# Attention with the probabilities scaled by 1/sum ahead of their transposes, in a two-layer hybrid transformer kernel

## The chip, the cores and the metric

One Trainium2 chip, one core of it. The metric is device time in microseconds (us) of one execution; of several runs the median is given. The engines are named as in the profile: PE (TensorE, with its weight loads as PEld), DVE (VectorE), ACT (ScalarE), POOL (GpSimd), and SP (SyncE, which issues the DMAs).

## The reference

Two layers over 1024 latent tokens (a 16 x 64 grid) and 256 context tokens of 1024 features, all in float32. The first layer mixes with neighbourhood attention (8 heads of 64) and a gated linear recurrence, the second with gated linear attention and grouped-query attention (8 query heads of 64 on 2 key heads). What the change touches are the two softmax attentions:

```python
# neighbourhood attention: 8 rows of keys around the query's row, 16 columns, and all of the context
p = softmax(concat([s_loc, s_ctx]))         # s_loc has the relative bias, -inf outside the window
o = einsum(p_loc, v_rows) + einsum(p[n_loc:], v_c)
# context queries of the first layer: the context alone
pc = softmax(q_c @ k_c.T * scale);  o_c = pc @ v_c
# grouped-query attention: context and all latents
p = softmax(q @ k.T * scale);  o = p @ v
```

## The kernel before

Products of float32 operands are made from two halves: each operand is a sum hi + lo in a short form, and a product is three matmuls (`mm3`, lines 128 to 133) or, in attention, two. The projections, with 512 columns per matmul, are most of the time.

Attention works in units of one head and 128 queries (`AttnUnit`). Neighbourhood attention has 80 of them: per head two of context queries, with 256 keys, and eight of latent queries, with 768 or 896 keys (four each). Grouped-query attention has 64, each with 1024 latent and 256 context keys. A unit goes through these methods:

- `scores` (L714): six or fewer matmuls into PSUM; VectorE copies the scores to SBUF (tiles `sc`) with the running maximum (L850 to L871, or L1519 and L1521).
- `exp` (L723): ScalarE takes the exponential in place and adds up the row sums into the small tile `st`.
- `norm` (L728, L729): VectorE adds the two sums where there are two tiles, and takes the reciprocal into `st[:, 7:8]`.
- `turn` (L738): TensorE transposes the probabilities, 128 keys each, into PSUM, up to four to a bank. With the last bank it also transposes the reciprocal, spread over 128 columns (L740), so that 1/sum lies along the columns; ScalarE copies that to SBUF (L741) into one of four buffers `rb` of the pool `recip`. ScalarE and VectorE then write the transposed probabilities as hi + lo into `pt` (L751, L752). For the third bank of every second unit of grouped-query attention the lo half is made by GpSimd (L747 to L749).
- `values` (L758): TensorE multiplies `pt` with the values, hi and lo of both, into one PSUM bank for two query tiles (`Pair`).

`run_attention` is a software pipeline over the units. In one step it issues the scores of unit n, `norm` of unit n-1, whatever closes an earlier pair, `turn` of unit n-3, `exp` of unit n, `values` of unit n-4, and then one step of the background generators and of a filler. The filler in both stages is the early half of the output projection: its weights are split on ScalarE and GpSimd (L90, L92), its matmuls run on TensorE (L131 to L133), and GpSimd adds its results to the residual (L1143), which goes back to DRAM. In neighbourhood attention GpSimd also adds masks to each next head's bias tables (L681, L684) ahead of the norm of the step in which they are issued; the tables come by DMA (L652).

`attn_out` closes a pair: ScalarE copies and VectorE adds the halves of the four partial products (L800, L801), GpSimd adds the two of each tile (L803, 64x256) and multiplies each tile by its 1/sum (L809, two of 64x128). In neighbourhood attention latent queries lie in reversed column order (`flip`), and the product writes them back in order.

Every engine works through its own instructions in the order in which the program issues them.

Of the kernel before, what the change touches and what calls it, by code (L numbers as in the profile page):

```python
# [10 lines left out]
F32 = mybir.dt.float32  # L11
# [20 lines left out]
class Emit:  # L32
    def __init__(self, ctx, tc, A, out, dbg):
# [7 lines left out]
        self.rp = e(tc.tile_pool(name="recip", bufs=4))  # L41
# [53 lines left out]
    def w_ahead(self, n_split, n_dma):  # L95
        """Keep n_split units split, and n_dma more loaded, beyond the units taken."""
        end = len(self.wplan)
        while self.wsp < min(end, self.wpos + n_split):
            self.w_load(self.wsp + 1)
            self.w_split(self.wsp)  # L100
            self.wsp += 1
        upto = min(self.wsp + n_dma, self.wpos + n_split + n_dma)

        def later():
            for _ in range(self.w_lag):
                yield
            self.w_load(upto)

        if self.w_lag:
            self.bg.append(later())  # L110
        else:
            self.w_load(upto)
# [15 lines left out]
    def mm3(self, ps, w, u, start, stop):  # L128
        """ps += w.T @ u with both operands given as (hi, lo)."""
# [5 lines left out]
    def split(self, hi, lo, src, scale=None, pool=False):  # L135
        """hi + lo = src (times a power of two): hi by ScalarE, lo by VectorE or GpSimd."""
# [9 lines left out]
class Act:  # L146
    """Feature-major activations in (hi, lo): per 128 features, tokens 1024 + 256."""
# [20 lines left out]
class Res:  # L168
    """Feature-major float32: per 128 features a [128, 1024] tile, and 256 more."""
# [40 lines left out]
def params(E):  # L210
    """Vectors over features: loaded as rows, turned into columns of one tile."""
# [35 lines left out]
class Mods:  # L247
    """mod[l][:, j] = (silu(c), silu(c_ctx)) @ w_mod[l][:, 1024 j:] + b_mod, features on partitions.

    A pass covers 1024 columns: ("b", l, j) a block, or ("h", l, hf) half hf of blocks 0 and 1."""  # L250
# [86 lines left out]
def make_gain(E, l, which, a, b):  # L337
    """gain = norm_w * (1 + scale)"""
# [9 lines left out]
def mod_part(E, src, r, u, k, c, gain, shift, pool=False):  # L348
    """u(hi, lo) = src * r * gain + shift, as a generator."""
# [17 lines left out]
def start(E):  # L367
    """x, ctx: row sums of squares, transposes, modulation and the norm of layer 0; x.T goes to DRAM."""
# [61 lines left out]
def proj_fm(E, w, u, cs, done):  # L430
    """Feature-major product of one 128-column unit w (hi, lo: [128, 8, 128]) for chunks cs.

    A generator of four steps per chunk; done(c, n, ps) may return a generator, run in the background."""
# [13 lines left out]
def col_units(key, ap, c0, n):  # L447
    """n units of 128 columns of a [1024, *] weight."""
# [12 lines left out]
def tick(E):  # L461
    """One step of every background generator."""
# [5 lines left out]
def store(E, dst, src, lag=4):  # L468
    """A store that is issued some background steps later, when its data is there."""
# [12 lines left out]
def pipe(gens, gap):  # L482
    """Software pipeline: a generator starts every gap steps, all started ones advance by one per step."""
# [54 lines left out]
def lru_tile(E, j, xl, gl, ct, o_d):  # L538
    """Conv, gates, both recurrences and the output gate of channels 128 j .. 128 j + 127."""
# [87 lines left out]
def na_bias_setup(E):  # L627
    """rpb rows padded to 127 columns in DRAM, so that a [64, 64] Toeplitz block is one strided read."""
# [14 lines left out]
def na_head_load(E, h, qk_d, v_d):  # L643
    """Bias tables and operands of head h."""
# [31 lines left out]
def na_head_mask(E, hd, i):  # L676
    """Quarter i of the masks of a head's bias tables."""
# [14 lines left out]
class AttnUnit:  # L692
    """One 128-query tile of one head.

    qs: (hi, lo) stationary operands [128, 128]; pieces: PSUM tiles of scores, each a list of moving APs;
    soft(pss, ss, st) writes the scores and returns a function that gives -max; groups: columns of each score tile;
    vtiles: stationary [128 keys, vh | vl] per key tile; o_ps() gives the PSUM columns of the output."""
# [27 lines left out]
    def norm(self):  # L725
# [3 lines left out]
        nc.vector.reciprocal(st[:, 7:8], st[:, 5:6])  # L729
        self.cols = [s[:, o:o + 128] for s, n in zip(self.ss, self.groups) for o in range(0, n, 128)]  # L730
        self.pts = []

    def turn(self, b):
# [5 lines left out]
        if b == self.nb - 1:  # L739
            nc.tensor.transpose(ps[:, m * 128:m * 128 + 128], self.st[:, 7:8].to_broadcast([128, 128]), E.ident)  # L740
            nc.scalar.copy(self.o_ps.recip(), ps[:, m * 128:m * 128 + 128])  # L741
# [20 lines left out]
def run_attention(E, units, fill=None, lag=3):  # L762
    """Software pipeline over the units of an iterator: norm 1, turn lag, values lag + 1 steps after the scores."""
# [30 lines left out]
def attn_out(E, pair, parity, dst, flip=False):  # L794
    """dst[64 rows at 64 * parity, two query tiles] = the four partial products of pair.ps [128, 2, 2, 128], times pair.r."""
# [7 lines left out]
    nc.gpsimd.tensor_tensor(v[:, :, 0], v[:, :, 0], v[:, :, 1], op=OP.add)  # L803
    for i in range(2):
        w, r, d = v[:, i, 0], pair.r[i][a], dst[:, i * 128:i * 128 + 128]
        if flip:
            w, r, d = (x.rearrange("p (r q) -> p r q", q=64) for x in (w, r, d))
            d = d[:, :, ::-1]
        nc.gpsimd.tensor_tensor(d, w, r, op=OP.mult)  # L809


class Pair:
    """The outputs of two query tiles in PSUM, and 1 / sums along their columns; taken at the first use."""

    def __init__(self, E):
        self.E, self.ps, self.r = E, None, {}
# [5 lines left out]
class Part:  # L822
# [8 lines left out]

    def recip(self):
        p = self.pair
        p.r[self.i] = p.E.rp.tile([128, 128], F32, name=p.E.nm("rb"), tag="rb")
        return p.r[self.i]
# [130 lines left out]
def mixer0(E, u, st, tail):  # L966
    """st: what is left of the norm that writes u; tail(O, h): what follows chunk 2."""
# [124 lines left out]
class Back:  # L1092
    """The residual read back from DRAM: ctx() its chunk 2, lat() chunks 0 and 1 of 128 features more."""
# [16 lines left out]
def faster(g, n):  # L1110
    """n steps of g as one."""
# [11 lines left out]
def out_plan(E, l, w, early, late, cs):  # L1123
    """Weights of an out projection, 256 columns at a time: rows from 128 * early once per chunk, then the others."""
# [6 lines left out]
def out_early(E, l, cs, load, back):  # L1131
    """h += gate * (O @ w_out) in DRAM, for the four feature tiles of O that load(c) brings; a generator.

    The sums are read back (back) once they are all there."""
# [55 lines left out]
def out_proj(E, l, O, h, c, W, fill, norm, ahead=0):  # L1190
    """h += gate * (O @ w_out) for chunk c and the four feature tiles of O; steps of fill run in between; a generator.

    norm, the norm of the result, takes a step after every tile of 128 features. ahead, for the last chunk: how many
    of the weights that follow are split meanwhile."""
# [26 lines left out]
def norm_mod(E, h, u, c, gain, shift, pool=False, lag=2, which=0):  # L1221
    """u = norm(h) * gain + shift for chunk c, as a generator; the first eight steps take h.part(0..7)."""
# [30 lines left out]
def ff_ops(cs, G=2):  # L1253
    """Order of the products of the hidden groups g: (1 or 2, group, chunk).

    Two chunks: two groups of the first one come first. Three chunks: the second one starts early. The last
    two groups end chunk 0 early."""
# [46 lines left out]
def ff(E, l, u, h, ops, G=2, fill=None, after=None, woven=False, slow=None, split=False):  # L1304
    """h += gate * (relu(u @ w1)^2 @ w2), as the given ops; fill, slow: run in between.
# [881 lines left out]
```

## Time and profile before

| | |
|---|---|
| median of 3 runs | 2994.69 us (2993.69 to 2995.0) |
| span of the profiled execution | 2993.8 us |
| TensorE busy | 2898.8 us (97%) |
| VectorE busy | 1605.6 us (54%) |
| ScalarE busy | 1195.7 us (40%) |
| GpSimd busy | 1076.7 us (36%) |
| neighbourhood attention | about 403 to 655 us of the span |
| grouped-query attention | about 1920 to 2242 us |

The profile is taken on one execution; its span runs from the first to the last instruction. Busy shares are means over stages with different limits, so the views by stretch say more than the page's totals. Durations of TensorE's instructions overlap; what an instruction takes of TensorE's time is read from one start to the next. In rows of groups, "x" is the count; behind the bar come the busy time in us and the mean in ns of one, and then the idle time before them with what ended it.

### The profile page before, as it was taken

To read this page: it belongs to the slowest core of one execution; us is meant where nothing else is said; L and a number is where in the kernel's file an instruction comes from. 1 tells how busy PE (TensorE), PEld (TensorE's weight loads), DVE (VectorE), ACT (ScalarE), POOL (GpSimd) and SP (SyncE) were. 2 spreads that over 40 slices of the span, in tenths; PEclk is the share of its full clock that TensorE was granted. 3 is DMA by queue.
4 is the path that set the end of the run, shared out by engine and by line. 5 is a ranking of instruction groups with operands and counts; after the bars stand their busy time and mean duration, and the time that the engine had idled before them with its cause. 6 is when DMAs were issued, how large, how long until landed. Compare 5 with 4: busy or idle time off the path is not lost. (4 is left out here: it accounts for less than half of the span.)

```text
span 2993.8 us, 43072 instructions
## 1 busy us (share of the span) xinstructions
PE 2898.8 (97%) x16517; PEld 2500.8 (84%) x16517; DVE 1605.6 (54%) x3309; ACT 1195.7 (40%) x2301; POOL 1076.7 (36%) x866
## 2 busy tenths in 40 slices
PE   7999999989999999999999998899999999999998
PEld 5797789978888888888888797789988888888887
DVE  5454458877434534534437566888886332323334
ACT  5654458864211112112125343578884112112122
POOL 1443347643332222223234334325545233323230
PEclk9999999999999999999999999999999999999999
DMA  7235698831221221321213221334411111111111
GB/s 253 86 113 193 222 246 230 232 97 43 71 64 50 71 78 51 105 71 57 84 43 125 86 78 39 103 106 139 142 45 58 43 57 43 57 43 50 49 57 57
DMA packets 235173, 286.98 MB, mean 96 GB/s; under 512 B 32656, under 2 KB 172760, under 8 KB 234968
## 3 DMA queue, kind: packets, MB, share of 16 engines
q1 hardware_dynamic: 234968, 284.24, 30.9%
q8 instruction: 130, 2.13, 0.3%
q14 instruction: 75, 0.61, 0.1%
HBM read 226.97 MB, written 57.23 MB: 95 GB/s over the span
## 5 line engine op out<-in xcount | busy, mean ns | idle before, releaser
L131 PE MATMUL ps<-act,whi 128*128 128x512 f32 (+1 forms) x2176 | 805.1, 370 | 6.5 <-ACT act L355 5.4
L132 PE MATMUL ps<-act,whi 128*128 128x512 f32 (+1 forms) x2176 | 800.5, 368 | 0.8 <-POOL act L361 0.7
L133 PE MATMUL ps<-act,wlo 128*128 128x512 f32 (+1 forms) x2176 | 798.6, 367 | 2.1 <-POOL wlo L92 1.2
L92 POOL TENSOR_TENSOR wlo<-wst,whi 128x1024 fp32r<-128x1024 f32 x190 | 465.7, 2464 | 408.6 <-ACT whi L90 282.6
L139 DVE TENSOR_TENSOR hid<-t,hid 128x512 fp32r<-128x512 f32 (+1 forms) x160 | 102.3, 639 | 793.1 <-ACT hid L138 793.1
L131 PEld LDWEIGHTS ps<-act,whi 128*128 128x128 f32 x2176 | 412.9, 190 | 78.3 <-issue 7.4
L131 PE MATMUL ps<-hid,whi 128*128 128x512 f32 (+1 forms) x1296 | 476.2, 367 | 0.0
L132 PE MATMUL ps<-hid,whi 128*128 128x512 f32 (+1 forms) x1296 | 474.4, 366 | 0.0
L133 PE MATMUL ps<-hid,wlo 128*128 128x512 f32 (+1 forms) x1296 | 474.2, 366 | 0.0
L133 PEld LDWEIGHTS ps<-act,wlo 128*128 128x128 f32 x2176 | 412.0, 189 | 70.5 <-POOL wlo L92 1.6
L132 PEld LDWEIGHTS ps<-act,whi 128*128 128x128 f32 x2176 | 412.9, 190 | 65.5 <-POOL act L361 1.3
L1345 POOL TENSOR_TENSOR t<-t 128x512 f32<-128x512 f32 (+1 forms) x160 | 153.7, 960 | 865.6 <-ACT t L1344 857.5
L1344 ACT ACTIVATE t<-ps 128x512 f32<-128x512 f32 (+1 forms) x160 | 88.7, 555 | 922.2 <-PE ps L133 922.1
L1363 DVE SCALAR_TENSOR_TENSOR hl<-ps,mod,hl 128x512 f32<-128x512 f32 (+1 forms) x520 | 371.0, 738 | 134.3 <-PE ps L133 131.2
L131 PEld LDWEIGHTS ps<-hid,whi 128*128 128x128 f32 x1296 | 245.1, 189 | 41.6 <-issue 1.6
L133 PEld LDWEIGHTS ps<-hid,wlo 128*128 128x128 f32 x1296 | 245.0, 189 | 39.6
L132 PEld LDWEIGHTS ps<-hid,whi 128*128 128x128 f32 x1296 | 245.2, 189 | 38.9
L90 ACT CAST whi<-wst 128x1024 fp32r<-128x1024 f32 x194 | 197.9, 1048 | 82.9 <-PE ps L132 37.6
L723 ACT ACTIVATE sc<-sc,st 128x1024 f32<-128x1024 f32 (+3 forms) x208 | 178.1, 859 | 32.2 <-DVE st L1524 23.8
L752 DVE TENSOR_TENSOR pt<-ps,pt 128x512 fp32r<-128x512 f32 (+2 forms) x304 | 169.1, 598 | 18.9 <-ACT pt L751 16.4
L751 ACT CAST pt<-ps 128x512 fp32r<-128x512 f32 (+2 forms) x304 | 153.4, 526 | 37.2 <-PE ps L738 29.8
L138 ACT CAST hid<-t 128x512 fp32r<-128x512 f32 (+1 forms) x160 | 92.5, 578 | 184.3 <-POOL t L1345 184.3
(326 smaller groups left out, 4187.9 us busy)
## 6 DMA issues: line engine op xcount, KB each, us to landing
wst<-in_w_ff SPq DMA_DIRECT2D x128, 512.0 KB
wm<-in_w_mod SPq DMA_DIRECT2D x96, 512.0 KB
wst<-in_w_in_even SPq DMA_DIRECT2D x20, 512.0 KB
wst<-in_w_in_odd SPq DMA_DIRECT2D x18, 512.0 KB
qk_d<-qks SPq DMA_DIRECT2D x16, 512.0 KB
wst<-in_w_out_even SPq DMA_DIRECT2D x16, 512.0 KB
qst<-qk_d SPq DMA_DIRECT2D x32, 256.0 KB
he<-h_d SPq DMA_DIRECT2D x32, 256.0 KB
```

The costliest lines, as they stand in the source:

```text
L90: self.nc.scalar.copy(hi, st)
L92: engine.tensor_tensor(lo, st, hi.bitcast(F32), op=OP.subtract)
L131: t.matmul(ps, w[0], u[0], start=start, stop=False)
L132: t.matmul(ps, w[0], u[1], start=False, stop=False)
L133: t.matmul(ps, w[1], u[0], start=False, stop=stop)
L138: self.nc.scalar.copy(hi, src)
L139: (self.nc.gpsimd if pool else self.nc.vector).tensor_tensor(lo, src, hi.bitcast(F32), op=OP.subtract)
L723: self.E.nc.scalar.activation(s, s, AF.Exp, bias=self.nm, accum_out=self.st[:, 5 + i:6 + i])
L751: nc.scalar.copy(pt[:, :, 0], src)
L752: nc.vector.tensor_tensor(pt[:, :, 1], src, pt.bitcast(F32)[:, :, 0], op=OP.subtract)
L1345: nc.gpsimd.tensor_tensor(r, r, r, op=OP.mult)
L1363: nc.vector.scalar_tensor_tensor(dst, ps[:, :n], gate[:, o, v:v + 1], dst, op0=OP.mult, op1=OP.add)
```

## The change

`norm` gets one GpSimd instruction per score tile, which multiplies the exponentials in place by the unit's 1/sum, one value per partition. The transposes then work on scaled probabilities. The broadcast transpose of the reciprocal (L740), its copy (L741), the buffers for it and `Part.recip` go. `attn_out` no longer multiplies: where the columns are in order, GpSimd's add of the two partial products of both tiles writes the output; where they are reversed, two adds, one for each tile, write it in order. The rest of the diff removes comments.

```diff
-        self.rp = e(tc.tile_pool(name="recip", bufs=4))
...
         nc.vector.reciprocal(st[:, 7:8], st[:, 5:6])
+        for s in self.ss:
+            nc.gpsimd.tensor_scalar(s, s, st[:, 7:8], None, op0=OP.mult)
         self.cols = [s[:, o:o + 128] for s, n in zip(self.ss, self.groups) for o in range(0, n, 128)]
...
-        if b == self.nb - 1:
-            nc.tensor.transpose(ps[:, m * 128:m * 128 + 128], self.st[:, 7:8].to_broadcast([128, 128]), E.ident)
-            nc.scalar.copy(self.o_ps.recip(), ps[:, m * 128:m * 128 + 128])
         pt = E.S([128, m, 2, 128], F32R, name="pt")
...
     v = t[a].rearrange("p (u s q) -> p u s q", u=2, s=2)
-    nc.gpsimd.tensor_tensor(v[:, :, 0], v[:, :, 0], v[:, :, 1], op=OP.add)
+    if not flip:
+        nc.gpsimd.tensor_tensor(dst.rearrange("p (u q) -> p u q", u=2), v[:, :, 0], v[:, :, 1], op=OP.add)
+        return
     for i in range(2):
-        w, r, d = v[:, i, 0], pair.r[i][a], dst[:, i * 128:i * 128 + 128]
-        if flip:
-            w, r, d = (x.rearrange("p (r q) -> p r q", q=64) for x in (w, r, d))
-            d = d[:, :, ::-1]
-        nc.gpsimd.tensor_tensor(d, w, r, op=OP.mult)
+        x, y, d = (z.rearrange("p (r q) -> p r q", q=64) for z in (v[:, i, 0], v[:, i, 1], dst[:, i * 128:i * 128 + 128]))
+        nc.gpsimd.tensor_tensor(d[:, :, ::-1], x, y, op=OP.add)
...
-    def recip(self):
-        p = self.pair
-        p.r[self.i] = p.E.rp.tile([128, 128], F32, name=p.E.nm("rb"), tag="rb")
-        return p.r[self.i]
```

## Rows read from the trace of the kernel before

**Rows 1.** The page: busy time of TensorE, and the chain that ended last by line.

```profile
PE 2898.8 (97%) x16517; PEld 2500.8 (84%) x16517; DVE 1605.6 (54%) x3309; ACT 1195.7 (40%) x2301; POOL 1076.7 (36%) x866
PE 32%; DVE 3%; issue 0%; ACT 0%; POOL 0%; DMA 0%; SPq 0%; DVEq 0%; POOLq 0%; ACTq 0%
```

**Rows 2.** Busy us (x instructions) of each engine by stretch, with granted clock and DMA.

```profile
core 0: us, PE busy (x) PEld busy (x) DVE busy (x) ACT busy (x) POOL busy (x), PEclk, DMA share, GB/s
425.00:590.00 165.00, 163.04 (x1206) 154.28 (x1205) 137.99 (x519) 141.77 (x334) 121.00 (x143) 1.00 0.90 233
...
2003.00:2166.00 163.00, 162.93 (x1093) 148.81 (x1094) 141.65 (x432) 140.78 (x329) 82.45 (x95) 1.00 0.43 133
2166.00:2210.00 44.00, 42.98 (x311) 38.89 (x309) 43.43 (x151) 42.65 (x106) 16.48 (x26) 1.00 0.23 67
```

**Rows 3.** The same view of the broadcast transposes (L740) alone: PE, PEld, clock, DMA.

```profile
425.00:590.00 165.00, 14.99 (x55) 7.53 (x55) 1.00 0.90 233
...
2003.00:2166.00 163.00, 9.00 (x33) 4.57 (x34) 1.00 0.43 133
2166.00:2210.00 44.00, 3.27 (x12) 1.60 (x12) 1.00 0.23 67
```

**Rows 4.** Timeline of the weight loads in grouped-query attention: start, us, instruction.

```profile
2101.80 0.14 PEld L740 LDWEIGHTS ps<-ident,st 128*128 128x128 f32 x1
2101.91 0.42 PEld L758 LDWEIGHTS ps<-pt,vl 128*128 128x128 f32 x3
```

**Rows 5.** Groups by line over the whole span: removed product and removed copy.

```profile
L809 POOL TENSOR_TENSOR ol<-t,rb 64x128 f32<-64x128 f32 x128 | 57.0, 464 | 5.0
...
L741 ACT COPY rb<-ps 128x128 f32<-128x128 f32 x144 | 39.8, 276 | 16.2 <-POOL oc L809 6.2 <-PE ps L740 5.2 <-POOL ol L809 4.1
```

**Rows 6.** Groups by line of GpSimd from 425 to 590 us.

```profile
L92 POOL TENSOR_TENSOR wlo<-wst,whi 128x1024 fp32r<-128x1024 f32 x10 | 24.0, 2396 | 6.4 <-ACT whi L90 6.3
...
L803 POOL TENSOR_TENSOR t<-t 64x256 f32<-64x256 f32 x27 | 19.8, 734 | 31.3 <-DVE t L801 26.0 <-ACT rb L741 4.4 <-POOL b L681 0.4
...
L684 POOL TENSOR_TENSOR braw<-braw,m 128x512 f32<-128x512 f32 x11 | 14.3, 1304 | 0.1
```

**Rows 7.** Groups by line of GpSimd over the span, three of 128x1024.

```profile
L92 POOL TENSOR_TENSOR wlo<-wst,whi 128x1024 fp32r<-128x1024 f32 x190 | 465.7, 2464 | 408.6 <-ACT whi L90 282.6 <-issue 46.1 <-DVE acc L285 32.4
...
L1697 POOL TENSOR_TENSOR ss<-ss,dec 128x1024 f32<-128x1024 f32 x4 | 7.6, 1896 | 22.8 <-DVE ss L1691 19.2 <-PE ps L133 3.5
...
L1966 POOL MEMSET att<- 128x1024 f32 x1 | 1.0, 957 | 0.0
```

**Rows 8.** Timelines: a unit's reciprocal and its transposes, in each attention.

```profile
500.84 0.16 DVE L729 RECIPROCAL st<-st 128x1 f32<-128x1 f32 x1
...
506.10 0.92 PE L738 MATMUL ps<-ident,sc 128*128 128x128 f32 x7
...
2107.08 0.16 DVE L729 RECIPROCAL st<-st 128x1 f32<-128x1 f32 x1
...
2115.59 1.26 PE L738 MATMUL ps<-ident,sc 128*128 128x128 f32 x10
```

**Rows 9.** Waits of ScalarE from 403 to 650 us: total, times, longest.

```profile
ACT rb L741 <- POOL oc L809: 6.2, 4, 2.4
...
ACT rb L741 <- POOL ol L809: 4.1, 6, 1.1
```

**Rows 10.** Timelines: a mask that waited for its table, and transposes after it.

```profile
418.78 0.88 POOL L681 TENSOR_TENSOR b<-braw,m 128x320 f32<-128x320 f32 x1 [19.65 <-DMA braw<-rpb_d]
...
420.34 0.93 PE L738 MATMUL ps<-ident,sc 128*128 128x128 f32 x7
```

**Rows 11.** Timeline of TensorE: the first transposes of the neighbourhood attention.

```profile
405.98 0.44 PE L738 MATMUL ps<-ident,sc 128*128 128x128 f32 x2 [0.37 <-ACT sc L723]
```

**Rows 12.** Timeline: a maximum on VectorE beside a subtraction on GpSimd.

```profile
2028.43 2.39 POOL L92 TENSOR_TENSOR wlo<-wst,whi 128x1024 fp32r<-128x1024 f32 x1 [4.04 <-ACT whi L90]
...
2029.07 1.77 DVE L1521 TENSOR_TENSOR st<-st 128x1 f32<-128x1 f32 x1
```

More of the change, by code (lines that the diff above doesn't have):

```diff
@@ L802, in attn_out @@
     v = t[a].rearrange("p (u s q) -> p u s q", u=2, s=2)
-    nc.gpsimd.tensor_tensor(v[:, :, 0], v[:, :, 0], v[:, :, 1], op=OP.add)
+    if not flip:
+        nc.gpsimd.tensor_tensor(dst.rearrange("p (u q) -> p u q", u=2), v[:, :, 0], v[:, :, 1], op=OP.add)
+        return
     for i in range(2):
-        w, r, d = v[:, i, 0], pair.r[i][a], dst[:, i * 128:i * 128 + 128]
-        if flip:
-            w, r, d = (x.rearrange("p (r q) -> p r q", q=64) for x in (w, r, d))
-            d = d[:, :, ::-1]
-        nc.gpsimd.tensor_tensor(d, w, r, op=OP.mult)
+        x, y, d = (z.rearrange("p (r q) -> p r q", q=64) for z in (v[:, i, 0], v[:, i, 1], dst[:, i * 128:i * 128 + 128]))
+        nc.gpsimd.tensor_tensor(d[:, :, ::-1], x, y, op=OP.add)
 class Pair:
     def __init__(self, E):
-        self.E, self.ps, self.r = E, None, {}
+        self.E, self.ps = E, None
     def part(self, i):
```

## The prediction

> **What bounds the kernel now.** I read the page first: TensorE is busy for 97% of the span, and the chain of work that ended last is all TensorE but for a few per cent of VectorE [rows 1]. So time is to be had only where TensorE gets less to do, or waits less. The change touches the two attention stages alone: the neighbourhood attention (NA, about 403 to 655 us of the span, 80 units of one head and 128 queries) and the grouped-query attention (GQA, about 1920 to 2242 us, 64 units). The table by stretches comes next, and it shows two regimes [rows 2]. From 425 to 590 us and from 2003 to 2166 us TensorE is busy for 163.0 of 165 and 162.9 of 163 us: what leaves TensorE there shortens the run. From 2166 to 2210 us VectorE is busy for 43.4 of 44 us: there it bounds, and TensorE's share is worth nothing. The column to keep in mind is POOL (GpSimd), since it receives the new work: 121.0 of 165 us in the NA stretch, 82.5 of 163 in the GQA stretch. It is 73% full in the first and 51% in the second.
>
> **What is removed.** Each unit loses one broadcast transpose of 1/sum (L740). What it occupies is read between starts, not from its duration, for weight loads and matmuls overlap: its weight load starts at 2101.80 us and the next instruction's at 2101.91, so 0.11 us [rows 4]. 55 units lie in the NA stretch and 33 in the GQA stretch [rows 3]: 88 x 0.11 = 9.7 us, all of it on the path. The other 144 - 88 = 56 units lie in the fill and drain of the stages, beside the gated linear attention, or in the VectorE-bound stretch; I credit a third of them, 56 x 0.11 / 3 = 2.0 us. Sum: -11.7 us.
>
> ScalarE loses the copy of that transpose, 144 x 0.276 = 40 us [rows 5]. ScalarE is not the bound (142 of 165 and 141 of 163 us [rows 2]), so its busy time is costed at nothing; TensorE's matmuls hide it. But that copy also waited for GpSimd to give back one of four buffers, 6.2 + 4.1 us in the NA stage [rows 9], and such a wait delays the copies that feed the next products. These waits go with the buffers; I put 1 us of them on the path, for TensorE is nearly always busy in the stretch. If that cover is gone, nothing is lost: the removed work is simply less.
>
> GpSimd loses the products with 1/sum (L809), 0.46 us a unit [rows 5]. In GQA the add of the halves stays as long as it is and now writes the output itself. The add of the halves (L803) was 0.73 us a pair, 27 times in the NA stretch [rows 6]. For NA's latent tiles, whose rows are written in reversed order, it becomes two adds in the shape of the old products, 2 x 0.46 = 0.92, so 0.18 us more a pair. In the NA stretch that makes at most 55 x 0.46 - 27 x 0.18 = 25.3 - 4.9 = 20.4 us less, in the GQA stretch 33 x 0.46 = 15.2 us less. At the very end of GQA the last pair's products also lie ahead of what follows; I credit 0.9 us for two of them.
>
> **What is added.** One GpSimd instruction per score tile scales it in place by a column of 1/sum: 256, 768 or 896 columns a unit in NA (two, four and four of ten units, 717 on average) and 1024 + 256 in GQA. The trace has no GpSimd instruction of this kind, so its price per column is bounded by others of GpSimd [rows 7]. From below: the fill of 128x1024, which writes but reads nothing, took 957 ns, 0.93 ns a column. From above: a subtraction that reads two full tensors took 2464 ns, 2.41 a column. Between them: the product of a tensor with a broadcast operand took 1896 ns, 1.85 a column. Below nothing is excluded, since it is an added instruction on a serial queue. I take 1.1 ns a column. The scaling has one stream to read and one to write, and the scalar is one value per partition, so nothing forces a second stream; that puts it near the fill. The ends stay for the range.
>
> The Trainium skill speaks of this price twice, in the page GPSIMD Engine Reference. In "4.1 Engine selection" it has operations with one input run at roughly line rate, and in "3.1 Elementwise" it gives 1.03 cycles an element for short bodies; at the 1.2 GHz of its specifications that is an estimate of 0.86 ns a column, by which the sum below would come out near 2983. The same paragraph calls 1.8 cycles the best case of a tight unrolled loop, an estimate of 1.5 ns, by which nothing would be left of the gain. No row here shows either for this instruction.
>
> What GpSimd then carries, against TensorE's shortened stretch: in NA 165 - 6 = 159 us, and 121.0 - 20.4 = 100.6 us plus 55 x 717 columns. At 0.93 ns that is 100.6 + 37 = 137 us, 86%; at 1.1, 144 us, 91%; at 1.85, 174 us, 109%; at 2.41, 196 us, 123%. In GQA, 163 - 4 = 159 us and 67.3 us plus 33 x 1280 columns: 107 us (67%) at 0.93, 114 (72%) at 1.1, 145 (91%) at 1.85, 169 (106%) at 2.41. NA decides.
>
> **The new wait.** The transposes now wait for GpSimd and not for ScalarE. The scaling can start when the reciprocal is done; the transposes of the same unit come two steps later. In NA that is 500.84 to 506.10 us, 5.3 us; in GQA 2107.08 to 2115.59, 8.5 us [rows 8]. GpSimd works in order, so what stands ahead of a scaling is the rest of the step before: a mask (1.3 us), a weight remainder (2.4 us) [rows 6], the adds (0.9 us). All of them in one step make 4.6 us, as much as is left of the 5.3 beside the scaling's own 0.8; what joins them is late, and one or two of them are not. Behind a late scaling stand all of TensorE's queue, the values of the unit before and the projection's matmuls. Ten weight remainders lie in the NA stretch, and a mask of either kind in two of five steps, so some four or five meetings; with a second remainder's or a mask's part of them late I take 0.6 us each: 3 us of new waits is my estimate, 1 us at the lower price and over 15 at the middle one, where the load is above 100%. The queue also waits for DMAs: a head's mask waited 19.7 us for its table, until 418.78, and ended at 419.66, where the transposes of the unit behind it started at about 420.3 [rows 10]. A scaling of 896 columns between them takes 1.0 us, so some 0.4 us late; it is part of the 3 us, and it would be 1 to 2 us a head, seven times, if tables came later.
>
> At the start of NA the pipeline is short: transposes start at 405.98 us, as soon as the exponentials are done [rows 11]. There the scaling of 256 columns lies on the path, for two units, and the first one of GQA is alike: 0.5 us each, 1.5 us in all.
>
> **Sum.** -11.7 - 1.0 - 0.9 + 3.0 + 1.5 = -9.1 us against the span of 2993.8: 2984.7. The median of the runs, 2994.69, is 0.9 us above the span, so I expect 2985.6, say 2985.5.
>
> **The rivals.** First, GpSimd becomes the bound (slower). If the scaling costs what a two-input operation costs, GpSimd needs 196 us in the NA stretch, 31 more than the 165 now, and 169 in GQA's, 6 more than now; the VectorE-bound stretch holds 12 units, 16.5 - 5.5 + 12 x 3.1 = 48 us of GpSimd in 44, 4 more. Less 3 us that are still won elsewhere: +38, 3033. It decides from about 1.9 ns a column on, where NA alone gives back more than the 13.6 us won. For it: most elementwise rows of GpSimd lie at 1.85 and above, all but the fills. Against it: all of those read two operands.
>
> Second, the gain is given back (no change). Between 1.3 and 1.85 ns a column NA's load is 95 to 109%, and the waits are 6 to 18 us against 13.6 won: 2989 to 3001, in the middle 2995. For it: the load is already 73% and comes in lumps.
>
> Third, VectorE is held up by GpSimd. A tiny maximum (L1521, two inputs in SBUF) began at 2029.07 us and ended at 2030.84, when a GpSimd subtraction that had begun at 2028.43 ended: 1.77 us for one value a partition [rows 12]. The Trainium skill, SBUF — State Buffer, "Who interferes with whom", states this rule: a VectorE instruction with two SBUF inputs is blocked by a GpSimd instruction that reads SBUF, for its whole length; the trace agrees. In the VectorE-bound stretch 12 units share 44 us [rows 2, 3], 3.7 us a step, and such a maximum comes once a step, just ahead of the reciprocal. GpSimd's step there is 16.5 / 12 - 0.46 = 0.9 us and a scaling of 1.4: done before the next maximum. From some 2.8 us of scaling on, 2.2 ns a column, or earlier if it starts late, they aren't, and 12 units lose about 0.8 us each: 10 us, 2995. It needs the scaling to be slow, or late, so it is small by itself.
>
> Fourth, the removed transposes don't shorten TensorE's stretches, because there something else ends last (VectorE is busy for 142 of 163 us, and for 138 of 165): 2993. Against it, TensorE has next to no idle time in them.
>
> **How the numbers follow.** Forecast 0.48 (its own range 2981 to 2989, from 0.93 to 1.3 ns); GpSimd the bound 0.22; gain given back 0.20; VectorE held up 0.05; nothing gained 0.05. A measurement of this kernel can tell about 0.2%, 6 us, from no change. Faster by more: nearly all of the forecast and the lower end of the second rival, 0.48. Within 0.2%: 2989 to 3001, most of the second rival, the third and the fourth, 0.26. Slower: the first rival and the end of the second, 0.26. The range goes from 2977 (the lowest price, all removed transposes paid) to 3014 (about 2.1 ns a column); it leaves out the far half of the first rival.
>
> **What would show it.** The new GpSimd rows: 128x1024 near 1.1 us and 128x896 near 1.0. TensorE's busy share in the NA stretch stays near 99% and the units come 0.11 us closer. If TensorE's transposes wait for GpSimd's scaling in the list of waits for more than some 5 us in all, the estimate of 3 us is wrong; over 12 us and the sign is. GpSimd near 100% in 425 to 590 us would be the first rival, a maximum of VectorE that lasts over 1 us in most units the third.

## The result: 4.3% slower, and GpSimd is the bound in both attentions

| | before | after |
|---|---|---|
| median of 4 runs | 2994.78 us | 3122.68 us (3120.58 to 3123.68) |
| span of the profiled execution | 2993.8 us | 3118.6 us |
| TensorE busy | 2898.8 us (97%) | 2922.2 us (94%) |
| GpSimd busy | 1076.7 us (36%) | 1417.1 us (45%) |

After over before is 1.0428, 95% interval 1.0413 to 1.0443. The forecast was 2985.5 us, with a range up to 3014. It was wrong in sign and by 137 us.

In the profile after, lines are shifted: L730 is the new scaling, L713 the scores, L739 the transposes, L747 the lo half that GpSimd makes, L749 and L750 the hi and lo halves of ScalarE and VectorE, L756 the values, L802 and L806 the adds that close a pair, L1513 the maximum of two columns in grouped-query attention. The first view is that of the groups of GpSimd by line and shape over the whole span (behind the bar: busy us, mean ns of one, idle time ahead and what ended it):

```profile
L730 POOL TENSOR_SCALAR sc<-sc,st 128x1024 f32<-128x1024 f32 x64 | 182.1, 2845 | 19.4 <-DVE st L1516 8.4 <-DVE st L728 4.7 <-ACT pt L746 2.6
...
L730 POOL TENSOR_SCALAR sc<-sc,st 128x896 f32<-128x896 f32 x32 | 80.7, 2523 | 0.3
...
L730 POOL TENSOR_SCALAR sc<-sc,st 128x256 f32<-128x256 f32 x80 | 73.8, 923 | 14.7 <-DVE st L728 7.7 <-DVE st L866 7.1
...
L730 POOL TENSOR_SCALAR sc<-sc,st 128x768 f32<-128x768 f32 x32 | 70.3, 2206 | 6.5 <-DVE st L850 4.1 <-PE ps L756 1.8 <-DVE st L728 0.6
```

The scaling of 128x1024 takes 2845 ns. The forecast had put 1.1 us on it and 2.41 ns a column as its upper bound; 2845 ns are 2.78 a column. The price is not only one of columns: 923 ns for 256 of them are 3.6 a column. All 208 scalings make 405 us, where 139,264 columns at 1.1 ns had been 153.

The busy time by stretch then shows what that does (columns as in [rows 2]: the stretch, its length, then busy us and count of TensorE, its weight loads, VectorE, ScalarE, GpSimd, then granted clock, DMA share and GB/s):

```profile
425.00:690.00 265.00, 207.67 (x1351) 190.12 (x1351) 168.48 (x622) 157.53 (x328) 248.24 (x195) 0.92 0.65 169
2060.00:2280.00 220.00, 190.00 (x1180) 168.30 (x1178) 161.98 (x494) 152.62 (x333) 211.76 (x142) 0.95 0.34 106
```

Against [rows 2] the roles have changed. GpSimd is busy for 248 of 265 us in neighbourhood attention (NA) and 212 of 220 in grouped-query attention (GQA); TensorE, 99% busy there before, has 78% and 86%. What TensorE waits for, in the list of its waits (total us, times, longest), the largest from 403 to 715 us and the largest from 1980 to 2370:

```profile
PE ps L739 <- POOL sc L730: 57.3, 36, 6.0
...
PE ps L756 <- POOL pt L747: 48.9, 25, 4.0
```

The second of these in the kernel before, over the whole span (there L758 is the values and L749 the lo half):

```profile
PE ps L758 <- POOL pt L749: 1.0, 4, 0.3
```

In NA the transposes wait for the scaling, as the forecast said they would, but for 57 us and not 3. In GQA they hardly do. There the values wait for the lo halves of L747, which stand behind the scalings in GpSimd's queue; before, that wait made 1.0 us in all.

One such step in NA in GpSimd's timeline (start us, length, instruction):

```profile
626.74 0.88 POOL L806 TENSOR_TENSOR ol<-t 64x128 f32<-64x128 f32 x2
627.69 1.28 POOL L1135 TENSOR_TENSOR he<-he 128x512 f32<-128x512 f32 x1
628.93 2.34 POOL L91 TENSOR_TENSOR wlo<-wst,whi 128x1024 fp32r<-128x1024 f32 x1
631.23 1.26 POOL L683 TENSOR_TENSOR braw<-braw,m 128x512 f32<-128x512 f32 x1
632.47 4.38 POOL L730 TENSOR_SCALAR sc<-sc,st 128x768 f32<-128x768 f32 x2
```

And TensorE's, from the last scores to the transposes that wait:

```profile
628.37 0.40 PE L713 MATMUL ps<-xst 128*128 128x256 f32 x2
634.73 1.54 PE L739 MATMUL ps<-ident,sc 128*128 128x128 f32 x6 [5.96 <-POOL sc L730]
```

GpSimd has no gap. Two adds, a residual add, a weight remainder and a mask stand ahead of the scaling, and TensorE's transposes wait 5.96 us for the end of the first of the two scalings in the last line. And it costs more than the wait, as the same stretch by windows shows:

```profile
630.00:635.00 5.00, 0.28 (x2) 0.28 (x3) 0.00 (x0) 0.00 (x0) 5.00 (x4) 0.89 0.10 39
635.00:640.00 5.00, 5.00 (x19) 4.52 (x19) 1.02 (x2) 3.13 (x7) 4.84 (x5) 0.50 0.32 99
```

After five microseconds in which TensorE was busy for 0.28, the granted clock is 0.50, the lower of its two levels (1.2 instead of 2.4 GHz), and it gets 19 matmuls done in 5 us.

The length of a stage is what the experiments are compared by. It is counted from the start of the first score product with latent keys to the start of the last value product with latent values (from the views of these two lines). The context parts of a stage lie up to 3 us outside.

| kernel | NA, us | GQA, us | median, us |
|---|---|---|---|
| before | 245.7 | 318.8 | 2994.8 |
| after | 311.2 | 382.6 | 3122.7 |
| after without the scaling | 237.2 | 313.4 | 2980.9 |
| change in GQA alone | 243.4 | 384.6 | 3061.9 |
| change in NA alone | 312.2 | 319.1 | 3056.8 |
| scaling as a product with a broadcast column | 270.4 | 330.3 | 3027.2 |
| the same, lo halves on VectorE | 269.2 | 324.2 | 3023.6 |
| copies in place of scalings | 242.9 | 319.0 | 2993.0 |
| the same, VectorE's maximum rewritten | 245.4 | 314.1 | 2986.8 |

Each length comes from one execution. Where NA's code is the same its length still differs, by 2.3 us (245.7 and 243.4) and 2.5 us (242.9 and 245.4), so a difference of that size in a stage says nothing.

### The profile page after: what moved, and what is told of

Read it like the earlier page. It is cut to its first block, busy times and chain, and to the rows that moved or that the text cites. A ratio compares the mean times of both kernels' runs of the same rounds, so it can differ in the third digit from the quotient of the medians.

```text
span 3118.6 us, 42860 instructions
## 1 busy us (share of the span) xinstructions
PE 2922.2 (94%) x16373; PEld 2511.5 (81%) x16373; DVE 1618.8 (52%) x3309; ACT 1174.6 (38%) x2157; POOL 1417.1 (45%) x962
## 5 line engine op out<-in xcount | busy, mean ns | idle before, releaser
L730 POOL TENSOR_SCALAR sc<-sc,st 128x1024 f32<-128x1024 f32 (+3 forms) x208 | 405.0, 1958 | 41.0 <-DVE st L728 12.9
L739 PE MATMUL ps<-ident,sc 128*128 128x128 f32 x1088 | 154.8, 286 | 65.6 <-POOL sc L730 59.5
L749 ACT CAST pt<-ps 128x512 fp32r<-128x512 f32 (+2 forms) x304 | 142.4, 523 | 151.2 <-PE ps L739 141.3
```

The source lines that it names most:

```text
L730: nc.gpsimd.tensor_scalar(s, s, st[:, 7:8], None, op0=OP.mult)
L739: nc.tensor.transpose(ps[:, t * 128:t * 128 + 128], self.cols[4 * b + t], E.ident)
L749: nc.scalar.copy(pt[:, :, 0], src)
```

## The experiments

The theory after the result: the price of one scaling makes GpSimd the bound of both attentions (load). Its rivals: the added step between reciprocal and transposes is one too many for the pipeline, whatever it costs (wait); GpSimd's reads hold VectorE up (port).

### What the removal is worth

```diff
-        for s in self.ss:
-            nc.gpsimd.tensor_scalar(s, s, st[:, 7:8], None, op0=OP.mult)
```

> The changed kernel without the scaling (so the attention outputs are left undivided by their sums): what the removed work is worth by itself. The prediction's terms for it are -11.7 (transposes), -1.0 (buffer waits), -0.9 (end): 2981, with 2978 to 2985. If TensorE's stretches don't get shorter (the fourth rival): 2993 to 2996.

Measured: 2980.89 us, 0.9945 of before (0.9929 to 0.9962). The removed transposes, waits and products are worth 14.1 us by the medians (the interval allows 11 to 21), where the forecast's terms gave 13.6. NA is 8.5 us shorter and GQA 5.4. So that half of the sum was right within the scatter, and the fourth rival is out: everything that was lost, 142 us, is the scaling.

### Load or wait

Two runs take the wait apart from the load. One moves the transposes a step further behind (lag 3 to 4); the other issues the scalings after the transposes, so that nobody needs them.

```diff
-def run_attention(E, units, fill=None, lag=3):
+def run_attention(E, units, fill=None, lag=4):
```

> The changed kernel with the transposes one step further behind the scores (lag 4 instead of 3), so three steps and not two for the scaling to be done. Load theory: no help, 3110 to 3130, for a queue that has over 100% to do is late by any distance. Wait theory: at least half of the loss comes back, 3060 or less.

```diff
     def norm(self):
...
-        for s in self.ss:
-            nc.gpsimd.tensor_scalar(s, s, st[:, 7:8], None, op0=OP.mult)
...
     def values(self):
+        for s in self.ss:
+            self.E.nc.gpsimd.tensor_scalar(s, s, self.st[:, 7:8], None, op0=OP.mult)
```

> The same scalings, of the same tiles, but issued with the values of a unit, so after its transposes have read the unscaled probabilities: nobody reads what they write (the outputs are undivided by their sums). GpSimd's load stays, TensorE's wait for the scaling goes. Load theory: GpSimd still has over 100% to do, and TensorE waits for its other work (masks, weight remainders, adds) instead: 3100 to 3125. Wait theory: 2980 to 3000.

Measured: 3120.98 us with the longer lag, which is no help at all, and 3165.77 us with the scalings that nobody reads. In NA the wait theory falls with both: the stage takes 303.1 us with the longer lag and 304.6 with scalings that nobody reads, against 311.2 in the changed kernel and 237.2 without the scaling, and GpSimd is busy for 260 and 252 of the 265 us from 425 to 690. In GQA, where the stage takes 391.6 and 414.4 us against 382.6, neither run is a clean test, for both bring waits for buffers (with the longer lag VectorE's score copies wait 49.0 us for one that GpSimd's closing add still reads). There the wait theory falls with the copies further down, which stand in the same place in the queue at a low price. That the second run is 43 us slower than the changed kernel I had not expected. The list of waits from 1980 to 2400 us says how:

```profile
ACT t L798 <- POOL sc L753: 102.7, 27, 6.0
DVE t L799 <- ACT t L798: 75.7, 27, 4.0
...
PE ps L737 <- DVE t L799: 28.4, 11, 3.2
```

L753 is the scaling in its late place, L798 the copy that closes a pair. The 256 context columns lie in one of six temporary buffers, which now stays taken until the scaling has run. So ScalarE waits 27 times for a buffer, VectorE's add L799 waits for ScalarE (75.7 us), and TensorE's next transposes for VectorE's add (28.4 us). A queue that has more to do than time finds another way to hold up TensorE when the first one is closed.

### One attention alone

> The change in grouped-query attention alone; neighbourhood attention as in the kernel before. Load theory: a unit needs 3.77 us of scaling beside 2.0 us of other GpSimd work (67.3 us for 33 units), 5.8 us, where TensorE needs 159/33 = 4.8; so this attention alone is bound by GpSimd, and about half of the 128 us show: 3045 to 3065. If only neighbourhood attention were bound, as its fuller GpSimd before suggests (73% against 51%): 2990 to 3000.

> The change in neighbourhood attention alone, grouped-query attention as in the kernel before. Load theory: GpSimd needs 100.6 us of other work and, for 55 units, some 11 x 0.92 + 22 x 2.21 + 22 x 2.52 = 114 us of scaling where TensorE needs 159, so it is bound; what grouped-query attention alone did not cost (64 of 128 us) shows here: 3053 to 3064. If one attention's delay had partly hidden the other's (weights, stores): over 3070 or under 3045.

Measured: 3061.94 us (ratio 1.0215) with the change in GQA alone, 3056.82 us (1.0211) in NA alone. The losses, 64 and 61 us against the runs of before beside them, make 125 of 128: each attention is bound by GpSimd for itself. That GQA, whose GpSimd was 51% full before, loses as much as NA at 73% fits its 1280 columns a unit, 3.77 us, against 717 columns and 2.1 us.

### The price by itself

```diff
...
+    for _ in range(3):
+        nc.gpsimd.tensor_scalar(a, a, col, None, op0=OP.mult)
+        nc.gpsimd.tensor_scalar(a, a, 1.0, None, op0=OP.mult)
+        nc.gpsimd.tensor_tensor(a, a, col.to_broadcast([128, 1024]), op=OP.mult)
+        nc.gpsimd.tensor_tensor(a, a, a, op=OP.mult)
+        nc.gpsimd.tensor_copy(d, a)
+        nc.gpsimd.tensor_scalar(d, a, col, None, op0=OP.mult)
...
```

> The kernel before, with six GpSimd instructions of 128x1024, three times each, ahead of its work, in data that nobody uses, and then three scalings each on VectorE and ScalarE: the price by itself. If reading the scalar from a column is what is dear, the scaling by a constant and the copy take about 960 to 1100 ns and the scaling by a column 2845, in place or not. If the one-scalar form is dear as such, all three of its variants take 2845. If it was contention in the attentions, the column form takes under 1900 here. The product with a broadcast column: 1896; two full inputs: 2460.

Measured, in the groups by line from 0 to 80 us; L218 to L223 are the six lines of the diff in order, L225 and L227 the same scaling on VectorE and ScalarE:

```profile
L218 POOL TENSOR_SCALAR pa<-pa,pr 128x1024 f32<-128x1024 f32 x3 | 8.5, 2844 | 0.3
L223 POOL TENSOR_SCALAR pd<-pa,pr 128x1024 f32<-128x1024 f32 x3 | 8.5, 2842 | 0.3
L219 POOL TENSOR_SCALAR pa<-pa 128x1024 f32<-128x1024 f32 x3 | 8.3, 2767 | 0.3
L220 POOL TENSOR_TENSOR pa<-pa,pr 128x1024 f32<-128x1024 f32 x3 | 5.7, 1892 | 0.2
L221 POOL TENSOR_TENSOR pa<-pa 128x1024 f32<-128x1024 f32 x3 | 5.7, 1892 | 0.2
L227 ACT ACTIVATE pd<-pd,pr 128x1024 f32<-128x1024 f32 x3 | 3.4, 1148 | 41.3 <-DVE pd L225 41.3
L222 POOL COPY pd<-pa 128x1024 f32<-128x1024 f32 x3 | 3.1, 1037 | 0.2
L225 DVE TENSOR_SCALAR pd<-pd,pr 128x1024 f32<-128x1024 f32 x3 | 2.3, 754 | 41.5 <-POOL pd L223 41.4
```

The one-scalar form is dear as such: with a column or a constant, in place or not, 2.77 to 2.84 us, and as much here, where VectorE is busy for 0.4 and ScalarE for 1.5 of 41 us (from 2 to 43 us), as in the attentions. It is not contention and not the reading of the column (0.08 us). A copy, one stream in and one out, takes 1037 ns; the same product with 1/sum as a broadcast second operand, so an operation with more to read, 1892.

The Trainium skill, GPSIMD Engine Reference, "4.1 Engine selection", has one-input operations at roughly line rate. The copy's row agrees and the one-scalar product's does not, so the measurement decides and the rule has to be read form by form.

### A cheaper form

```diff
-            nc.gpsimd.tensor_scalar(s, s, st[:, 7:8], None, op0=OP.mult)
+            nc.gpsimd.tensor_tensor(s, s, st[:, 7:8].to_broadcast([128, s.shape[-1]]), op=OP.mult)
```

> The scaling becomes a two-input product with the column of 1/sum read as a broadcast operand (in the kernel before, such a product of 128x1024 took 1896 ns; the scaling by a pointer took 2845). Load theory (GpSimd's price per column makes it the bound of both attentions): the 208 scalings go from 405 us to some 260 to 270, the time falls by most of these 135 us, to 2985 to 3015; GpSimd stays near 100% in the NA stretch and below in GQA. Wait theory (a step of GpSimd between reciprocal and transposes is one too many for the pipeline, whatever it costs): at most a third comes back, 3080 or more. Port theory (VectorE is held up by GpSimd's reads): the second input makes it no better, 3100 or more.

Measured: 3027.21 us (1.0103; 1.0085 to 1.0121). The scalings take 270.7 us instead of 405, and 95 of the 128 us come back, as the load theory wants. But the time lies 12 us above the top of what was expected, and of these 12 no run tells the cause. GpSimd's groups over the span have the price:

```profile
L730 POOL TENSOR_TENSOR sc<-sc,st 128x1024 f32<-128x1024 f32 x64 | 121.3, 1896 | 43.6 <-DVE st L1516 29.3 <-DVE st L728 5.2 <-ACT pt L749 3.3
...
L730 POOL TENSOR_TENSOR sc<-sc,st 128x256 f32<-128x256 f32 x80 | 49.0, 614 | 16.9 <-DVE st L728 10.0 <-DVE st L866 6.9
```

And TensorE's list of waits has what is left:

```profile
PE ps L739 <- POOL sc L730: 23.7, 19, 4.6
PE ps L756 <- POOL pt L747: 14.5, 16, 1.9
```

The second wait is the one in GQA (counted at the weight loads of the same products it is 17.9 us, the 18 of the expectation below). The lo halves went to VectorE, to see whether they are the cause there:

```diff
-            nc.gpsimd.tensor_tensor(pt[:, :, 1], f, pt.bitcast(F32)[:, :, 0], op=OP.subtract)
+            nc.vector.tensor_tensor(pt[:, :, 1], f, pt.bitcast(F32)[:, :, 0], op=OP.subtract)
```

> The broadcast-column form in both attentions (3027 us), with the lo halves of the third bank on VectorE again and no longer queued behind GpSimd's scalings. If the 18 us of waits for these halves are what grouped-query attention lost there: 3008 to 3017. If they only mark a queue that is late anyway, and the transposes wait in their place: 3022 to 3030.

Measured: 3023.62 us (1.0092; 1.0077 to 1.0107), so the second case, if not by its whole account: GQA is 6.1 us shorter in the profiled runs (330.3 to 324.2), of the 14.5 waited. The medians are 3.6 us apart, which is not clear of the scatter. NA, where GpSimd has over 100% to do even at this price (76 us of scaling beside the 100.6 of the forecast, in 159), keeps its loss.

### Another engine, or shared

The scaling on VectorE (`nc.vector.tensor_scalar`, else as the changed kernel):

> The changed kernel with the scaling on VectorE instead of GpSimd. A VectorE product of 128x1024 by a column took 933 ns in the kernel before, 0.91 a column. Load theory, for VectorE: 138 + 36 = 174 us in the neighbourhood stretch where TensorE needs 159, 142 + 38 = 180 in the grouped-query one, 14 more in the stretch that VectorE bounds already: 2981 + 15 + 21 + 14 and as much again per unit outside these stretches: 3015 to 3060. If what costs is the added step between reciprocal and transposes, whatever the engine: 3100 or more. If VectorE's price is that of half a column (two a cycle): 2985 to 3000.

Measured: 3073.34 us (1.0256; 1.0239 to 1.0273), above the 3060 expected. VectorE's groups have the reason:

```profile
L730 DVE TENSOR_SCALAR sc<-sc,st 128x1024 f32<-128x1024 f32 x64 | 55.0, 859 | 2.2
L730 DVE TENSOR_SCALAR sc<-sc,st 128x896 f32<-128x896 f32 x32 | 34.3, 1073 | 1.1
L730 DVE TENSOR_SCALAR sc<-sc,st 128x256 f32<-128x256 f32 x80 | 34.3, 429 | 0.6
```

896 columns take longer than 1024, while 1024 alone took 754 (above): part of the price is waiting, most in NA, where GpSimd works most. Two scalings of 256 columns in VectorE's timeline show it:

```profile
496.96 3.04 DVE L730 TENSOR_SCALAR sc<-sc,st 128x256 f32<-128x256 f32 x1
502.20 0.35 DVE L730 TENSOR_SCALAR sc<-sc,st 128x256 f32<-128x256 f32 x1
```

GpSimd's work from 496 to 503 us:

```profile
...
496.22 1.29 POOL L1135 TENSOR_TENSOR he<-he 128x512 f32<-128x512 f32 x1
497.48 2.37 POOL L91 TENSOR_TENSOR wlo<-wst,whi 128x1024 fp32r<-128x1024 f32 x1
```

The first scaling begins inside the one GpSimd instruction and ends 0.15 us after the next, the second has GpSimd idle beside it. It is so for all 80 of NA: those with no GpSimd instruction beside them took 0.35, 0.62 and 0.69 us (256, 768 and 896 columns), the others 1.06, 1.39 and 1.37 in the mean. VectorE is then busy for 160 of the 165 us and 158 of the 163 us of [rows 2], where it had 138 and 142 before: a scaling at a third of GpSimd's price still fills it.

The change in GQA alone, with the 1024 latent columns on GpSimd as a broadcast product and the 256 context columns on ScalarE after its work of the step:

> Only grouped-query attention is changed, and its scaling is shared: GpSimd multiplies the 1024 latent columns with a broadcast column (1892 ns measured alone), ScalarE the 256 context columns, after its other work of the step (1147 ns for 1024 columns measured alone, so some 0.3 to 0.45 us). Load theory: GpSimd 67 + 33 x 1.9 = 130 us where TensorE needs 159, 82%; ScalarE gives up as much as it takes. What is won is grouped-query attention's share of the 14 us that the kernel without scaling won, some 6, less waits for the lo halves behind a scaling, some 5: 2988 to 2998. If the point from which GpSimd holds TensorE up lies well below full load: 3003 or more.

Measured: 2996.58 us, 1.0002 (0.9994 to 1.0011). Nothing lost, nothing won; TensorE waited 6.9 us for the lo halves (9.9 counted at the weight loads). With these on VectorE:

> The shared scaling in grouped-query attention alone (2996.6 against 2995.8 of before), with the lo halves of the third bank on VectorE instead of GpSimd. TensorE waited 9.9 us for these halves. If VectorE, at 142 of 163 us, takes 16 x 0.5 us in that stretch without becoming late: 2988 to 2993. If VectorE or ScalarE (148 of 163) hold the transposes up in their place: 2994 to 3000.

Measured: 2999.61 us, 1.0009 (1.0001 to 1.0018): the other case. No version with a real scaling beat the kernel before by more than the scatter.

### The forecast with its own premise

```diff
-            nc.gpsimd.tensor_scalar(s, s, st[:, 7:8], None, op0=OP.mult)
+            nc.gpsimd.tensor_copy(s, s)
```

> The changed kernel with each scaling replaced by a GpSimd copy of the tile onto itself (so the outputs are left undivided by their sums): the same tiles, the same place in the queue, the same waits, at 1037 ns for 128x1024, 1.01 a column, where the prediction had assumed 1.1. If the price per column is the one term that failed, the prediction's own sum holds here: 2980 to 2990. If its estimate of the waits (3 us) or of what stands behind a scaling failed as well: 2993 to 3005.

Measured: 2993.04 us, 0.9988 (0.9979 to 0.9997). The copies take 154.5 us in all, 1.11 ns a column, so the assumed 1.1 to the letter. (They need no reciprocal and may start a little earlier than a scaling.) The sum gave 2985.5; 7.5 us are missing. VectorE's groups over the span, the maximum of two columns, first in the kernel without the scaling:

```profile
L1511 DVE TENSOR_TENSOR st<-st 128x1 f32<-128x1 f32 x64 | 24.3, 379 | 0.0
```

With the copies:

```profile
L1513 DVE TENSOR_TENSOR st<-st 128x1 f32<-128x1 f32 x64 | 41.7, 651 | 0.0
```

One value a partition takes 651 ns in the mean beside the copies against 379 without (383 in the expectation that follows, over a shorter stretch), and 0.15 us at best. A timeline of GpSimd in the kernel with copies, around one of the long ones:

```profile
2030.29 2.40 POOL L91 TENSOR_TENSOR wlo<-wst,whi 128x1024 fp32r<-128x1024 f32 x1 [3.75 <-ACT whi L89]
2032.63 1.40 POOL L730 COPY sc<-sc 128x1024 f32<-128x1024 f32 x2
```

The same moment on VectorE:

```profile
2030.62 2.08 DVE L1513 TENSOR_TENSOR st<-st 128x1 f32<-128x1 f32 x1
```

It ends as the subtraction ends, as in [rows 12]. With the copies GpSimd reads more of the time, so more of these are long. To separate this from the queue, the maximum and the sum beside it were written so that they read one tensor and a column:

```diff
-        nc.vector.tensor_tensor(st[:, 3:4], st[:, 0:1], st[:, 1:2], op=OP.max)
+        nc.vector.tensor_scalar(st[:, 3:4], st[:, 0:1], st[:, 1:2], None, op0=OP.max)
...
-            nc.vector.tensor_tensor(st[:, 5:6], st[:, 5:6], st[:, 6:7], op=OP.add)
+            nc.vector.tensor_scalar(st[:, 5:6], st[:, 5:6], st[:, 6:7], None, op0=OP.add)
```

> The kernel with copies in the place of the scalings (outputs undivided), with two tiny VectorE operations of grouped-query attention, the maximum and the sum of two columns, written as one-scalar operations, which read one tensor and a column, not two tensors. If GpSimd's copies cost the 5.6 us of grouped-query attention by holding up that maximum (651 ns in the mean against 383 without the copies): the maximum falls under 220 ns and the time from 2993.0 to 2985 to 2989. If the copies cost it by their place in GpSimd's queue alone: 2991 to 2995.

> The kernel before with the same two operations rewritten and nothing else. The maximum took 463 ns in the mean, 64 times; at some 190 ns VectorE has 17 us less to do, of which what lies in its bound stretch counts (12 units x 0.27 = 3 us): 2990 to 2993. If the rewritten forms wait just the same: 2994 to 2998.

> The shared scaling in grouped-query attention alone (2996.6), with the same two operations rewritten. GpSimd reads more there, so more of the maximum is wait: 2989 to 2993. If ScalarE (148 of 163 us) or GpSimd's lo halves are what is left: 2994 to 2998.

Measured: with the copies 2986.82 us (0.9972; 0.9962 to 0.9981); in the kernel before 2994.71 (0.9999; 0.9991 to 1.0008); in the shared version 2994.26 (0.9996; 0.9987 to 1.0005). The maximum, in the groups of the first of the three:

```profile
L1513 DVE TENSOR_SCALAR st<-st 128x1 f32<-128x1 f32 x64 | 13.3, 208 | 0.0
```

GQA went from 319.0 to 314.1 us, next to the 313.4 without any scaling. So the copies cost GQA nothing but this maximum, 5 to 6 us. In the kernel before the same edit is worth nothing that can be measured: the 16 us that VectorE saves there on the maximum (463 to 209 ns, 64 times) do not show in the time. The expectation of 3 us for its bound stretch was a miss, and so was that of a gain for the shared version.

The Trainium skill, SBUF — State Buffer, "Who interferes with whom", has a VectorE instruction with two SBUF inputs blocked by a GpSimd instruction that reads SBUF; 651 ns against 208 agrees. The price that the rule has depends on what VectorE bounds: 6 us with the copies, nothing before.

## Why the prediction was wrong, point by point

**What bounds the kernel**: right for the two stretches of [rows 2], though the chain in [rows 1] carries less than was read from it. It covers 35% of the span, 32% TensorE and 3% VectorE, and says nothing of the rest.

**The removal** (-11.7, -1.0, -0.9): right, 14.1 us measured against 13.6.

**The price of the scaling**: the step that failed. It was bounded by other instructions of GpSimd [rows 7], a fill from below and a two-input subtraction from above, and 1.1 ns a column was chosen because "the scaling has one stream to read and one to write". That reason holds for a copy (1.01). It says nothing of the arithmetic: this form costs 2.78 a column, above the upper bound, which stood on two streams costing more than one. Why the form is so dear, no run tells. No row of before had this instruction on GpSimd, and the choice between ends that lay apart by 2.6 times decided the sign.

**The load sum**: its method was right. In the changed kernel's two stages GpSimd's work fills most of the length (the view by stretch):

```profile
401.00:713.00 312.00, 245.36 (x1629) 224.90 (x1630) 207.27 (x765) 191.25 (x395) 287.12 (x223) 0.92 0.63 167
1982.00:2366.00 384.00, 322.90 (x2125) 290.17 (x2120) 291.12 (x894) 255.03 (x583) 342.73 (x230) 0.96 0.26 83
```

The scalings alone, in the same stretches (here the columns behind the length are GpSimd, clock, DMA):

```profile
401.00:713.00 312.00, 165.63 (x80) 0.92 0.63 167
1982.00:2366.00 384.00, 239.36 (x128) 0.96 0.26 83
```

In NA 121 us of other work and 166 of scaling make 287 of 312 us, in GQA 103 and 239 make 343 of 384; for the rest, 25 and 41 us, GpSimd is idle, in GQA mostly at the ends of the stage, outside the stretch from 2060 to 2280 us shown at the start. Without the scaling the stages took 237 and 313 us. The prediction's own sum for its first rival, with the measured price in it, would have been NA 100.6 + 114.2 = 215 us in 165, GQA 67.3 + 33 x 3.77 = 192 in 163, and 11 + 12 x 3.77 = 56 in the 44 of the VectorE-bound stretch: +50, +29, +12, less 3, so +88 and 3083. Of the other 40 us it had no count: 25 and 19 units lie outside its stretches, and the clock fell. How much each makes, no run tells apart.

**The first rival** (GpSimd becomes the bound, 0.22): this is what happened, with its place and its sign: GpSimd 94 and 96% busy, transposes waiting in NA. What it lacked besides the price is the lower clock. Against the kernel without scaling the span is 136.7 us longer (3118.6 - 2981.9). TensorE, with the same number of instructions, is busy for 37.2 of these (2922.2 - 2885.0) and idle for the other 99.5. So about a quarter of the loss is TensorE being busy longer with the same work, which fits the window of granted clock 0.50 above.

**The new wait** (3.0 + 1.5 us): right in kind, but somewhat small even at the price assumed. TensorE's lists of waits have, with the copies, and then with the copies and the rewritten maximum:

```profile
PE ps L739 <- POOL sc L730: 5.9, 5, 2.1
```

```profile
PE ps L739 <- POOL sc L730: 7.9, 6, 2.7
```

Both are over the 5 us at which the prediction had called its estimate wrong. With the copies and the maximum out of the way, 2986.8 is 1.3 us off the forecast. That it comes so near is in part luck: the wait is larger, the removal gave a little more, and the maximum, which the sum had put at nothing, is rewritten. The wait's account named TensorE's queue behind a late scaling, and overlooked who else stands behind it on GpSimd itself: the lo halves of the third bank, which made 48.9 of the waits in GQA.

**The point from which it decides** ("about 1.9 ns a column on") lies lower. At 1.94 (270.7 us over 139,264 columns) the loss is already 32 us, at 1.11 there is a gain of 2 to 3. No run lies between, so the second rival's stretch, 1.3 to 1.85, is untested.

**The third rival** (VectorE held up, from 2.2 ns on) did not show in the changed kernel: its maximum took 424 ns in the mean against 463 before. The sum of two columns behind it did get longer, 305 ns against 150. Why the maximum collides no more often there, with GpSimd busier, no run tells. It showed where I had not looked for it, at the forecast's own price, and took 6 of the 9 us that I had thought won.

**The range** ended at 3014 because it left out "the far half of the first rival"; the time lies beyond that rival's own price.

## What to carry to other kernels

An instruction whose form is not in the trace on that engine has no price from its count of streams: measure it alone, or let the range hold what it does to the engine at the dearest row of that engine and beyond. When work goes to an engine that is half idle, sum its queue over the whole stage, and ask what else stands in that queue that others wait for. Scaling what is small beats scaling what is large: 1/sum on the outputs cost 0.46 us of GpSimd, 0.28 of ScalarE and 0.11 of TensorE a unit, on 1280 probabilities a row 3.77 us.

## What the runs showed of the hardware

GpSimd's product with one scalar (2767 to 2844 ns for 128x1024) is dearer than the same product with a broadcast second operand (1892) and 2.7 times a copy (1037). Two inputs that are one tile took 1892 as well, where the weight remainder, whose two inputs are different tiles, takes 2464 [rows 7]. VectorE did the scaling of 128x1024 in 754 ns alone and needed 859 for it in the mean in GQA. In NA 896 columns took 0.69 us with GpSimd idle and 1.37 in the mean with GpSimd at work; the rewritten maximum of 128x1, which reads one tensor and a column, took 199 to 215 ns beside GpSimd's copies, where the form with two tensors took up to 2190.
